# A mixture-of-experts layer on one core: bounded row transfers, paired down rows and another order of the last three experts

## The chip, the cores and the metric

The kernel runs on one core of a Trainium2 chip. The metric is device time in microseconds of one launch; the number given is the median of several runs. One further execution is recorded by the hardware profiler, and all rows below come from it.

## The reference

A decoder layer on 512 tokens of width 1024. A mixer (gated DeltaNet heads and sliding-window attention) comes first and is not touched here. Then each token is sent to 4 of 32 experts, and each expert is a clamped SwiGLU with weights of its own, all in float32:

```python
hu = xb @ w_up[e] + b_up[e]                  # 1024 -> 2048
x_glu = minimum(hu[:, :1024], 7.0)
x_lin = clip(hu[:, 1024:], -7.0, 7.0)
act = x_glu * sigmoid(1.702 * x_glu) * (x_lin + 1.0)
y = act @ w_down[e] + b_down[e]              # 1024 -> 1024
out[token] += gate[token, e] * y             # 4 experts a token
```

`w_up` is 8 MB an expert and `w_down` 4 MB, so the experts' weights are 384 MB, each used once.

## The kernel before, in words

The first 430 us or so compute the mixer, the router and the lists of rows. The experts' part follows, and there the change lies.

**Order and size.** Which expert has how many rows is known only at run time. The experts are ranked by their count, and the table `NB` gives each rank a fixed number of blocks of 32 rows: 7, 5, 5, 4, 4, 4, nine times 3, fourteen times 2, twice 1, and 4 for expert 0. `SEQ` is the order in which sizes are worked on, and `ORDER` turns it into ranks. Rows beyond a rank's blocks would go to a loop at the end (L1947 on), which did not run a pass here. An expert's rows are cut into units of 64 and, where the number of blocks is odd, one of 32 (`units`). A unit fills 128 partitions by cutting the columns in halves (64 rows) or quarters (32 rows).

**Rows in and out.** `gather` (L1685 on) makes an indirect DMA on GpSimd for each 128 rows: row numbers `gi` pick rows of `h2d` in DRAM and put them into `xg`, up to 128 partitions of 4 KB, with three buffers. Slots of the list that no token fills point at zero rows behind row 511. `turn` (L1694 on) transposes `xg` on TensorE for use as weights. At the end `put` (L1792 on) multiplies the result by gates and adds it to `out` in DRAM with an indirect DMA that accumulates, 128 pieces of 2 KB (64-row units) or 1 KB (32-row units). Unfilled slots add to rows behind row 511, which nobody reads. A scatter reads and writes `out`, so each waits until the one before it has landed; GpSimd holds the queue for that.

**Weights.** All weight loads are issued on the SP queue in chunks of 1 MB into 16 slots used in turn (`wslot`). `load_up` (L1640 on) loads eight chunks of 128 rows, where a partition receives one row of 8 KB. `load_down` (L1653 on) loads four chunks of 256 rows; chunk by chunk, partition p receives rows p and 128 + p, two runs of 4 KB. A chunk is issued when TensorE is done with the chunk that had its slot before.

**The loop.** Step q (L1904 on) loads `up(q+1)` and then `down(q)`, and on TensorE runs `up_pass(q)` (L1736 on), within it the transposes of the activations of q−1 (`turn_act`, L1769 on, after step 3) and of the rows of q+1 (`turn`, after step 5), and then `down(q−1)` (L1778 on) with its `put`. The gather for expert q+2 is issued in step q. The last step has only `down` and `put` of the last expert. TensorE, VectorE, ScalarE and SP keep the order that is written; GpSimd's is chosen by a scheduler.

`turn_act` cuts the activations' columns into pieces of 128 and transposes each, so that piece f holds rows 128f to 128f + 127 of `w_down`'s product; it has to match the order in which `load_down` put the rows on partitions.

## Time and profile before

| | us |
|---|---|
| median of 3 runs | 1517.06 (1514.83 to 1518.03) |
| the profiled execution | 1512.75 |
| its span, first to last instruction | 1510.9 |
| TensorE (PE) busy | 1384.6 (92%) |
| VectorE (DVE) busy | 563.1 (37%) |
| ScalarE (ACT) busy | 238.1 (16%) |
| GpSimd (POOL) busy | 225.4 (15%) |

Busy time counts instructions on an engine; SP's part, issuing DMAs, is not counted. Matmuls overlap one another and their ends are modelled, so a busy TensorE need not be at its peak. "DMA share" is the time that packets took as a share of 16 DMA engines; it goes over 1 where packets of several queues overlap. The granted clock is the share of full speed at which TensorE was allowed to run. Queue 1 (hardware_dynamic) carries the loads issued on SP, queue 0 (software_dynamic) what GpSimd issues, and so the gathers and scatters.

### The profile page before, as it was taken

The page shows a single profiled execution, that of the slowest core. Times are in us where ns is not written, and L with a number is a line of the kernel's source. Part 1 is how long each engine was busy: PE and PEld are TensorE (multiplying, and loading weights), DVE is VectorE, ACT ScalarE, POOL GpSimd, SP SyncE. Part 2 cuts the span into 40 slices and gives each one's busy share as a digit, 9 for nine tenths or more (in the row PEclk, how much of TensorE's full clock was granted, in tenths as well). Part 3 has the DMA queues.
Part 4 walks back from the last instruction along what each step waited for, and adds up shares of the span by engine and source line. Part 5 has one row for each costly group of instructions (what it writes and reads, how often), then busy time and mean ns, then how long its engine had stood idle before and what let it go on. Part 6 is the DMA issues. An engine that isn't in the chain of part 4 may idle for free. (4 is left out here: it accounts for less than half of the span.)

```text
span 1510.9 us, 22164 instructions
## 1 busy us (share of the span) xinstructions
PE 1384.6 (92%) x8586; PEld 595.2 (39%) x8586; DVE 563.1 (37%) x1247; ACT 238.1 (16%) x542; POOL 225.4 (15%) x181
## 2 busy tenths in 40 slices
PE   4999999999879999978999999999989999999764
PEld 3766656764433333222333333333233333343111
DVE  7865567465744213112221231233221332132110
ACT  4353354431111000000000000000000000010000
POOL 2213143101320110110011011111010111101001
PEclk9999999999979999999999999999999999999987
DMA  9656210256358999999999999999999999999996
GB/s 304 199 196 216 94 50 8 65 209 264 140 206 316 383 403 392 399 410 410 412 406 396 399 401 388 398 397 397 400 397 357 402 351 383 385 402 406 403 418 223
DMA packets 121363, 482.94 MB, mean 320 GB/s; under 512 B 10870, under 2 KB 37686, under 8 KB 88482
## 3 DMA queue, kind: packets, MB, share of 16 engines
q1 hardware_dynamic: 108226, 453.16, 76.3%
q0 software_dynamic: 11952, 25.54, 7.2%
q10 hardware_dynamic: 1072, 2.70, 0.5%
q8 instruction: 75, 1.23, 0.3%
q14 instruction: 38, 0.31, 0.1%
HBM read 464.14 MB, written 17.22 MB: 319 GB/s over the span
## 5 line engine op out<-in xcount | busy, mean ns | idle before, releaser
L1751 PE MATMUL ps_up<-we,xTe 128*64 128x512 f32 (+1 forms) x3040 | 622.0, 605 | 31.1 <-DMA we<-in_w_up_dram 27.4
L1787 PE MATMUL ps_dn<-we,aT 128*64 128x512 f32 (+1 forms) x1848 | 318.5, 535 | 31.5 <-DMA we<-in_w_down_dram 23.8
L1751 PEld LDWEIGHTS ps_up<-we,xTe 128*64 128x64 f32 (+1 forms) x3040 | 186.9, 131 | 407.0 <-issue 335.2
L1787 PEld LDWEIGHTS ps_dn<-we,aT 128*64 128x64 f32 (+1 forms) x1848 | 103.2, 129 | 248.4 <-issue 185.4
L1795 POOL DMA_INDIRECT out_dram<-yv,si x52 | 81.5, 1568 | 703.8 <-DVE yv L1794 533.1
L1703 DVE COPY xTe<-ps_xTe 128x256 f32<-128x256 f32 (+3 forms) x35 | 17.5, 500 | 308.8 <-PE ps_xTe L1702 308.8
L1775 ACT COPY aT<-ps_aT 128x512 f32<-128x512 f32 (+1 forms) x52 | 26.0, 531 | 532.7 <-PE ps_aT L1773 529.0
L1760 DVE TENSOR_TENSOR hu<-ps_up,bb 128x512 f32<-128x512 f32 (+1 forms) x52 | 32.1, 617 | 201.1 <-PE ps_up L1751 201.1
L1794 DVE SCALAR_TENSOR_TENSOR yv<-ps_dn,sg,g2p 128x512 f32<-128x512 f32 x38 | 28.5, 751 | 207.9 <-PE ps_dn L1787 207.0
L1762 ACT ACTIVATE hu<-hu 128x512 f32<-128x512 f32 (+1 forms) x52 | 29.9, 574 | 269.6 <-DVE hu L1761 269.6
L1690 POOL DMA_INDIRECT xg<-h2d,gi x35 | 33.3, 953 | 210.9 <-PE ps_xTe L1702 157.7
L317 PE MATMUL ps_ch<-hhi,wih 128*128 128x512 f32 x128 | 58.9, 460 | 0.0
L317 PE MATMUL ps_ch<-hl,wih 128*128 128x512 f32 x128 | 51.0, 399 | 0.0
L317 PE MATMUL ps_ch<-hhi,wl 128*128 128x512 f32 x128 | 50.8, 396 | 0.0
L1711 DVE STREAM_SHUFFLE bb<-bias 128x1024 f32<-128x1024 f32 (+1 forms) x44 | 48.7, 1134 | 0.1
L1703 ACT COPY xTe<-ps_xTe 128x256 f32<-128x256 f32 (+3 forms) x35 | 15.2, 434 | 170.6 <-PE ps_xTe L1702 170.6
L1702 PEld LDWEIGHTS ps_xTe<-cst,xg 64*128 64x128 f32 (+3 forms) x280 | 24.8, 144 | 30.8 <-issue 25.3
L1161 PE MATMUL ps_y<-wod,oT 128*128 128x512 f32 x64 | 35.2, 641 | 0.0
L1702 PE MATMUL ps_xTe<-cst,xg 64*128 64x64 f32 (+3 forms) x280 | 30.8, 252 | 3.2 <-PEq L1745 1.8
L317 PEld LDWEIGHTS ps_ch<-hhi,wih 128*128 128x128 f32 x128 | 24.2, 189 | 23.2 <-issue 18.0
L1142 PE MATMUL ps_y<-wos,oS 128*128 128x512 f32 x64 | 33.3, 613 | 0.0
L1766 DVE SCALAR_TENSOR_TENSOR act<-act,hu 128x512 f32<-128x512 f32 (+1 forms) x52 | 32.2, 620 | 1.8
(391 smaller groups left out, 1337.2 us busy)
## 6 DMA issues: line engine op xcount, KB each, us to landing
we<-in_w_up_dram SPq DMA_DIRECT2D x256, 1024.0 KB
we<-in_w_down_dram SPq DMA_DIRECT2D x128, 1024.0 KB
wa<-in_w_ada_dram SPq DMA_DIRECT2D x16, 512.0 KB
wi<-in_w_in_dram SPq DMA_DIRECT2D x8, 1024.0 KB
wl<-in_w_ada_dram SPq DMA_DIRECT2D x12, 512.0 KB
oS<-in_w_ada_dram SPq DMA_DIRECT2D x10, 512.0 KB
LL<-in_w_ada_dram SPq DMA_DIRECT2D x10, 512.0 KB
wt<-in_w_in_dram SPq DMA_DIRECT2D x4, 776.0 KB
```

Of the source, the lines that this page charges most:

```text
L317: TE.matmul(acc, lhsT=w[a], rhs=x_[b], start=start and q == 0, stop=stop and q == 2)
L1142: TE.matmul(a, lhsT=oS[:, j, P * i:P * i + P], rhs=wo[j][:, 512 * hf:512 * hf + 512], start=(j == 0), stop=(j == 3))
L1161: TE.matmul(a, lhsT=state["oT"][:, j, P * i:P * i + P], rhs=wo[4 + j][:, 512 * hf:512 * hf + 512], start=(j == 0), stop=(j == 3))
L1690: state["gather"] = G.indirect_dma_start(out=xg[:rows_], out_offset=None, in_=h2d, in_offset=bass.IndirectOffsetOnAxis(ap=gidx(g)[:rows_], ...
L1702: TE.transpose(pt[:, k, :rows_], xg[:rows_, 512 * hf + P * k:512 * hf + P * k + P], ident[:rows_, :rows_])
L1703: state["turned", hf] = (S.copy if hf else V.tensor_copy)(xt_[:, 4 * hf:4 * hf + 4, :rows_], pt[:, :, :rows_])
L1711: V.stream_shuffle(bbs[w].rearrange("p h n -> p (h n)"), b[w], [0] * 32)
L1751: TE.matmul(t[w * j:w * j + w], lhsT=lhsT, rhs=rhs, start=(k == 0), stop=(k == KT - 1))
L1760: V.tensor_tensor(g, pg, bbs[w][:, 0], op=OP.add)
L1766: V.scalar_tensor_tensor(l, l, 1.0, g, op0=OP.add, op1=OP.mult)
L1787: TE.matmul(py[u][w * j:w * j + w, 0:m], lhsT=aT[u][:, kt % nf, w * (kt // nf):w * (kt // nf) + w], rhs=wd[kt][:, m * j:m * j + m], start= ...
L1795: G.indirect_dma_start(out=outv[u[1]], out_offset=bass.IndirectOffsetOnAxis(ap=sidx, axis=0), in_=yv, in_offset=None, compute_op=OP.add)
```

## The change

There are four edits.

1. `SEQ` ends in 3, 1, 1 and no longer in 1, 3, 1: the expert of three blocks is worked on before both experts of one block.
2. The gather is bounded to rows 0 to 511 and the scatter to pieces of these rows. What points beyond is left out without an error. Since the partitions of `xg` that receive no row would hold old data, a memset of `xg` on GpSimd stands ahead of each gather.
3. `load_down` puts rows 2p and 2p + 1 of a chunk on partition p, one run of 8 KB.
4. `turn_act` picks the matching columns for each transpose: every second column of a group of 256, first the even ones, then the odd ones.

```diff
-SEQ = [..., 5, 2, 2, 1, 3, 1]
+SEQ = [..., 5, 2, 2, 3, 1, 1]
...
     def load_down(dn):
...
-            nc.sync.dma_start(t, dn[P * kt:P * kt + 256].rearrange("(f p) n -> p f n", p=P))
+            nc.sync.dma_start(t, dn[P * kt:P * kt + 256].rearrange("(p f) n -> p f n", f=2))
...
+            G.memset(xg[:rows_], 0.0)
             state["gather"] = G.indirect_dma_start(
-                out=xg[:rows_], out_offset=None, in_=h2d, in_offset=bass.IndirectOffsetOnAxis(ap=gidx(g)[:rows_], axis=0))
+                out=xg[:rows_], out_offset=None, in_=h2d, in_offset=bass.IndirectOffsetOnAxis(ap=gidx(g)[:rows_], axis=0),
+                bounds_check=T - 1, oob_is_err=False)
...
     def turn_act(u, l):
...
-        for a in range(0, m, P):
-            TE.transpose(pt[:, a:a + P], l[:, a:a + P], ident)
+        lv = l.rearrange("p (g q f) -> p g f q", f=2, q=P)
+        for a in range(m // P):
+            TE.transpose(pt[:, P * a:P * a + P], lv[:, a // 2, a % 2], ident)
...
         G.indirect_dma_start(out=outv[u[1]], out_offset=bass.IndirectOffsetOnAxis(ap=sidx, axis=0),
-                             in_=yv, in_offset=None, compute_op=OP.add)
+                             in_=yv, in_offset=None, compute_op=OP.add, bounds_check=T * D // m - 1, oob_is_err=False)
```

## Rows read from the trace of the kernel before

**Rows 1.** The page: DMA busy in 40 slices (tenths), queue 0's packets, MB, share.
```profile
DMA  9656210256358999999999999999999999999996
...
q0 software_dynamic: 11952, 25.54, 7.2%
```

**Rows 2.** Stretches: us, busy PE, PEld, DVE, ACT, POOL, granted clock, DMA share, GB/s.
```profile
488.00:1121.00 633.00, 601.22 (x3314) 201.00 (x3311) 160.11 (x311) 42.01 (x81) 67.14 (x52) 0.99 1.02 399
1121.00:1250.00 129.00, 128.03 (x699) 44.52 (x694) 39.12 (x96) 8.54 (x16) 15.73 (x13) 1.00 0.98 373
1250.00:1396.00 146.00, 141.72 (x726) 52.50 (x718) 38.19 (x73) 11.21 (x23) 18.78 (x14) 1.00 1.03 394
1396.00:1490.00 94.00, 69.55 (x412) 19.38 (x414) 16.97 (x39) 4.83 (x11) 6.21 (x4) 0.85 1.02 412
```

**Rows 3.** Waits of PE, 488 to 1121 us: total us, times, longest.
```profile
PE ps_dn L1787 <- DMA we<-in_w_down_dram: 16.7, 12, 3.8
PE ps_up L1751 <- DMA we<-in_w_up_dram: 12.7, 17, 1.7
```

**Rows 4.** Waits of PE, 1396 to 1490 us.
```profile
PE ps_up L1751 <- DMA we<-in_w_up_dram: 14.7, 14, 1.8
PE ps_dn L1787 <- DMA we<-in_w_down_dram: 7.2, 8, 1.5
```

**Rows 5.** Waits of the SP queue for TensorE, 1121 to 1396 us.
```profile
SPq L1649 <- PE ps_dn L1787: 27.8, 10, 7.3
...
SPq L1649 <- PE ps_up L1751: 24.0, 13, 8.6
```

**Rows 6.** Queue 0 (packets, MB, share) in 488:1121, 1250:1396 and 1396:1490.
```profile
q0 software_dynamic: 6480, 14.55, 9.7%
...
q0 software_dynamic: 1712, 3.28, 10.3%
...
q0 software_dynamic: 576, 0.79, 4.8%
```

**Rows 7.** Stretches of up chunks (first) and of down chunks; columns as rows 2.
```profile
1466.30:1473.70 7.40, 4.07 (x24) 0.52 (x24) 0.00 (x0) 0.00 (x0) 0.00 (x0) 0.79 1.00 420
1445.80:1453.30 7.50, 4.08 (x48) 1.43 (x48) 3.63 (x9) 0.42 (x1) 0.00 (x0) 0.79 1.04 426
1414.30:1421.80 7.50, 5.81 (x24) 1.45 (x24) 0.87 (x3) 0.00 (x0) 0.00 (x0) 1.00 1.03 425
```

**Rows 8.** Timeline of POOL and DVE at the end: start, us, what, idle before.
```profile
1488.23 1.55 POOL L1795 DMA_INDIRECT out_dram<-yv,si  x1 [30.52 <-DVE yv L1794]
1495.73 1.55 POOL L1795 DMA_INDIRECT out_dram<-yv,si  x1 [5.95 <-DVE yv L1794]
1500.00 1.55 POOL L1795 DMA_INDIRECT out_dram<-yv,si  x1 [2.71 <-DMA out_dram<-yv,si]
...
1495.18 0.48 DVE L1794 SCALAR_TENSOR_TENSOR yv<-ps_dn,sg,g2s 128x256 f32<-128x256 f32 x1 [6.83 <-PE ps_dn L1787]
```

**Rows 9.** Landing times: the scatter of L1795, then the gather into xg.
```profile
DMA to landing us min/median/max: 3.8/9.0/10.3
...
DMA to landing us min/median/max: 6.4/8.7/11.7
```

**Rows 10.** Transposes: L934 (strided source) and L1773 (contiguous); ns min/median/max.
```profile
L934 PE MATMUL ps_tm<-cst,kT x16: 272/273/329, 117.0 to 286.6; 128*128 128x128 f32 x16
...
L1773 PE MATMUL ps_aT<-cst,act x180: 272/273/476, 465.9 to 1487.8; 128*128 128x128 f32 x180
```

**Rows 11.** POOL's memsets of the bias tiles; POOL's first gather in the timeline.
```profile
L1681 POOL MEMSET bias<- x4: 539/752/967, 440.4 to 442.2; 128x512 f32 x2, 128x1024 f32 x2
...
431.39 1.05 POOL L1690 DMA_INDIRECT xg<-h2d,gi  x1 [7.51 <-DVE gi L1537]
```

**Rows 12.** GB/s of all DMA from 1480 to 1511 us in 40 slices.
```profile
GB/s 423 423 423 407 423 423 418 423 412 407 418 418 433 362 328 304 185 95 21 11 0 21 11 137 32 21 0 0 40 120 9 0 11 0 0 0 0 0 0 0
```

**Rows 13.** Timeline of PE: eight products of the last expert's up pass, twice.
```profile
1468.77 1.07 PE L1751 MATMUL ps_up<-we,xTe 128*32 128x512 f32 x8 [1.35 <-DMA we<-in_w_up_dram]
1471.21 1.93 PE L1751 MATMUL ps_up<-we,xTe 128*32 128x512 f32 x8 [1.38 <-DMA we<-in_w_up_dram]
```

## The prediction

> **What bounds the kernel now.** The page comes first: from the fourteenth of its forty slices on, the experts' part, the DMA row stands at 9 [rows 1]. The table by stretch says the same in numbers: DMA share 1.02 from 488 to 1121 us, 0.98 to 1250, 1.03 to 1396, 1.02 to 1490, while TensorE is busy for 601 of 633, 128 of 129, 142 of 146 and 70 of 94 us [rows 2]. Both engines are nearly full, so the waits decide who leads where. Up to 1121 us TensorE waits 16.7 + 12.7 = 29.4 us for weights [rows 3]. From 1121 to 1396, with the expert of seven blocks, that list has no wait for weights; the DMA queue waits instead for TensorE to free slots (27.8 + 24.0 us are its largest such rows) [rows 5]. From 1396 on TensorE waits again, 14.7 + 7.2 us [rows 4]: the weight stream sets the end. So what shortens DMA work counts in full only after about 1250 us, where the queue was last throttled (share 0.98 before it); earlier it counts where TensorE waits, and between 1121 and 1250 not at all. After the stream comes a tail of its own, in the timeline: the last product is read out at 1495.18, but its scatter starts at 1500.00, because the scatter of 1495.73 has to land first, and that one had waited for the scatter of 1488.23 [rows 8].

> **The order of the last experts.** Before, the last expert but one has three blocks and so two scatters, chained by their landings; the last expert's is third in the chain. Then the last but one has one block and one scatter. It starts about four down chunks before the last one's, four times 1.05 MB at 425 GB/s = 9.9 us [rows 7], and a scatter lands 9.0 us after issue in the median, 10.3 at most [rows 9]: at most 0.4 us are left to wait. The last scatter then starts where the readout ends, at 1495.73 and not at 1500.00: −4.3 us. Two things are late next. The three-block expert's second scatter now runs before the end of the stream. Queue 0 spends 4.5 us on 576 packets from 1396 to 1490 [rows 6], four scatters of 128 rows and 16 completions, 1.1 us each; this one has rows of half a pair, so I take 0.5 us. And TensorE has two experts of one block at the end: the same eight products took 1.07 us in one chunk and 1.93 in the next [rows 13], with the granted clock at a mean of 0.85 in that stretch [rows 2]; the last chunk of before took 1.07, so up to 0.9 us come on, taken as 0.4. Together −3.4, between −4.3 and −1.9. The weights themselves are the same bytes, and TensorE's blocks are the same number.

> **The bounded transfers.** The table NB gives 90 blocks, 2880 rows; 512 tokens times 4 choices are at most 2048 rows in use, so at least 832 of 2880, 28.9%, are moved for nothing, by gathers and by scatters. Queue 0, which carries both, takes 9.7% of 633 us = 61.4 us up to 1121, 10.3% of 146 = 15.0 us, and 4.8% of 94 = 4.5 us of all 16 engines' time [rows 6]. 28.9% of the last two is 5.6 us. Early it is 17.7 us, less than the 29.4 us that TensorE waits there [rows 3]. Bounds: nothing, if a skipped row costs as much as a moved one or if no engine that matters is relieved; 5.6 + 17.7 = 23.3 us if all counts. I take 5.6, the late part whole and the early part at nothing: TensorE's waits up to 1121 are 5% of that stretch, so most of what is saved there fills slots that the queue then waits for [rows 5], and what does get through I set against rows that are shared unevenly among the engines.

> Bounding may make the instruction or the making of its descriptors longer; no row has a bounded one. The nearest rows are the unbounded ones' landing times, 8.7 us for a gather and 9.0 for a scatter in the median [rows 9]. Both only lie on the path at two places: the first gather, which TensorE waits for at the start, and the last scatter. I take 0; the ends are no cost and a doubling, 17.7 us for the two, and below nothing is possible too, as fewer rows land sooner, in the range's 1 us.

> The 35 memsets go to GpSimd, up to 0.97 us each [rows 11]. The gather then waits for the memset ahead of it, and scatters queue behind both. The first has 7.5 us of idle GpSimd ahead of it [rows 11]; the others are issued up to two experts ahead, and an expert is 12 chunks of 1.05 MB at 420 GB/s [rows 7], 30 us, against a landing of 11.7 at most [rows 9]. Cost 0 behind that cover; were it gone, 1 us per gather that TensorE waits for.

> **Down rows in pairs.** A down chunk becomes 128 runs of 8 KB, as an up chunk is. Rows 7 compare stretches of one kind: up chunks come at 420 GB/s with share 1.00, down chunks at 426 and 425 with 1.04 and 1.03. By bytes delivered nothing is won. By share per byte a down chunk costs 1.04/426 against 1.00/420, 2.5% more; the ten late experts' 42 MB take 2.38 us per MB, 100 us, so that would be 2.5 us. I take 0, the rate being what TensorE sees; ends 0 and −2.5. [...]

> The transposes of the activations now read every second element as weights. L934 already transposes with a strided source (two heads interleaved), in 273 ns in the median, as L1773 does on contiguous data [rows 10]. So 0; the far end, twice the time for 180 of them, would be 49 us and has no row behind it.

> **Sum.** −3.4 − 5.6 = −9.0 us. The profiled execution took 1512.75 us (span 1510.9 and 1.85 around it), 4.3 below the median of 1517.06; it becomes 1503.8, the median 1508.1, said as 1508. The forecast's own range is 1503 to 1512. A difference under 0.2%, 3 us, is about what a measurement of this kernel can't tell from none.

> **Rivals.**
> *Only the tail gains.* The rows in use are the first of every transfer. If each engine gets a run of neighbouring rows, the first engines keep all of theirs, and the stream waits for them. For it: at the end of the stream the rate falls in steps from 433 to 95 GB/s over some 4 us [rows 12], so the engines do not finish together. Against it: nothing tells which rows go to which engine. The time: 1517.06 − 3.4 = 1513.7, just on the line of 0.2%. It is also the time if a skipped row still costs its slot in the queue, the case that bounding does not do what it says. [...] Chance 0.25.

> *The early savings count as well.* TensorE's 29.4 us of waiting [rows 3] fall by about half of the 17.7 us saved there, and the whole second half shifts. −3.4 − 5.6 − 8 = −17, 1500. For it: the waits are there; against it: slots fill. Chance 0.13.

> *Slower: bounded transfers land late.* If the check of every row makes a bounded transfer land x us later, the first gather and the last scatter add 2x on the path, and it decides from 2x above 9.0, x = 4.5, half of today's landing. Doubled, +17.7 − 9.0: 1525.8. For it: POOL's transfers take 9 us for little data, so making them is the larger part; against it: one comparison a row. Chance 0.12.

> **How the numbers follow.** Forecast 0.50, tail only 0.25, early too 0.13, slower 0.12. Tail only falls on both sides of the line, half and half: faster 0.50 + 0.13 + 0.12 = 0.75, same 0.13, slower 0.12. The range takes in the forecast, the early case and the tail case with its own spread: 1498 to 1516; outside it lie the slower case and a part of the early one.

> **What would show it.** The tail: two scatters after the last but one expert's readout and no idle GpSimd "DMA out_dram" before the last. The bound: of 2880 gathered and 52 × 128 = 6656 scattered rows 28.9% go, some 2750 of queue 0's 11952 packets [rows 1]. If its packets are as many as before, or TensorE's waits after 1396 stay at 22 us with fewer packets, the second term falls. Down rows: packets under 8 KB fall by 128 × 256 = 32768 for the down rows alone, and stretches of down chunks keep 425 GB/s. The forecast is wrong if TensorE's part ends where it did, or if landing times rise above 9 us.

## The result, and the profile after

| | before | changed |
|---|---|---|
| median of 4 runs each, us | 1515.94 (1511.09 to 1518.03) | 1491.98 (1486.96 to 1492.84) |
| ratio, 95% interval | | 0.9843 (0.9818 to 0.9868) |
| profiled execution; its span | 1512.75; 1510.9 | 1486.96; 1485.2 |

The change takes 24 us off, 1.6%; forecast were 9 us, and the measured time is 6 us below the range. Two of the edits did more than was forecast of them: the bounded transfers and the paired down rows.

The page of the changed kernel, DMA packets and queues; against it the same line of before (queue 0 of before is in [rows 1]):

```profile
DMA packets 104980, 476.16 MB, mean 321 GB/s; under 512 B 13992, under 2 KB 39556, under 8 KB 55714
...
q1 hardware_dynamic: 91842, 453.16, 77.0%
q0 software_dynamic: 11952, 18.75, 5.4%
```

```profile
DMA packets 121363, 482.94 MB, mean 320 GB/s; under 512 B 10870, under 2 KB 37686, under 8 KB 88482
...
q1 hardware_dynamic: 108226, 453.16, 76.3%
```

Packets under 8 KB are 32768 fewer: the down rows, as forecast. Queue 0 has 6.8 MB less and 5.4% instead of 7.2%, but exactly as many packets. Packets under 512 B are 3122 more. The router's choices for the reference's inputs leave 832 of 2880 gathered rows and 2290 of 6656 scattered pieces without a token, and that is 3122: what is left out keeps its packet. In the packet records a scattered piece becomes a packet of 8 bytes (2290 more of these on queue 0) and a gathered row one of 4 bytes (832 more); their median time is 9 ns, against 176 ns for a piece of 2 KB, 101 for one of 1 KB and 159 for a row of 4 KB.

The changed kernel by stretch (columns as [rows 2]), then what TensorE waited for from 488 to 1121 us and from 1396 to 1470, then queue 0 (packets, MB, share) from 1250 to 1396 and from 1396 to 1470:

```profile
488.00:1121.00 633.00, 609.78 (x3362) 208.02 (x3356) 159.95 (x312) 42.52 (x82) 90.08 (x73) 1.00 1.01 400
1121.00:1250.00 129.00, 127.69 (x696) 45.53 (x693) 37.71 (x91) 9.16 (x18) 19.19 (x17) 1.00 0.95 372
1250.00:1396.00 146.00, 141.81 (x723) 52.90 (x721) 40.39 (x77) 10.93 (x22) 21.81 (x17) 1.00 1.02 408
1396.00:1470.00 74.00, 56.51 (x366) 16.13 (x370) 13.74 (x33) 3.84 (x10) 6.21 (x4) 0.82 1.00 409
```

```profile
PE ps_dn L1792 <- DMA we<-in_w_down_dram: 11.7, 11, 3.1
PE ps_up L1755 <- DMA we<-in_w_up_dram: 9.0, 12, 1.8
...
PE ps_up L1755 <- DMA we<-in_w_up_dram: 10.5, 10, 1.9
...
PE ps_dn L1792 <- DMA we<-in_w_down_dram: 2.2, 4, 0.7
```

```profile
q0 software_dynamic: 1665, 1.78, 6.0%
...
q0 software_dynamic: 636, 0.42, 3.4%
```

TensorE's waits for weights fall from 29.4 to 20.7 us early [rows 3] and from 21.9 to 12.7 late [rows 4], 18 us in all. Late, queue 0 moves 2.20 MB instead of 4.07 [rows 6], 46% less and not 28.9%, at about as many packets (2301 and 2288): the last experts of the order have the emptiest blocks. Next come three points in time, the first down product of all (on PE, 475.55), the first of the expert of seven blocks (1184.24) and the last readout (on DVE, 1473.54), and the last scatter (on POOL):

```profile
475.55 1.46 PE L1792 MATMUL ps_dn<-we,aT 128*64 128x512 f32 x6
...
1184.24 1.51 PE L1792 MATMUL ps_dn<-we,aT 128*64 128x512 f32 x6
...
1473.54 0.48 DVE L1799 SCALAR_TENSOR_TENSOR yv<-ps_dn,sg,g2s 128x256 f32<-128x256 f32 x1 [10.05 <-PE ps_dn L1792]
...
1474.30 1.55 POOL L1800 DMA_INDIRECT out_dram<-yv,si  x1 [8.99 <-DVE yv L1799]
```

```profile
478.13 1.46 PE L1787 MATMUL ps_dn<-we,aT 128*64 128x512 f32 x6
...
1197.08 1.51 PE L1787 MATMUL ps_dn<-we,aT 128*64 128x512 f32 x6
```

The second fence is before. Between these points: 718.95 us before, 708.69 after, 10.3 less early; then to the last readout 298.10 (to 1495.18, [rows 8]) and 289.30, 8.8 less late. The last scatter now starts right behind the readout and waits for no landing: from readout to the end of the span 15.7 us before and 11.7 now, 4.1 less. The part ahead of the experts varies by some us from one execution to the next (the first gather of the executions recorded here was issued between 426 and 434 us), so lengths between such points compare better than times from the start. The choice of the first point matters too: counted from the first gather (431.39 [rows 11] and 427.16) the early gain is 8.6 us.

### The profile page after: what moved, and what is told of

It reads as the page before. It is cut to its first block, busy times and chain, and to the rows that moved or that the text cites. A ratio compares the mean times of both kernels' runs of the same rounds, so it can differ in the third digit from the quotient of the medians.

```text
span 1485.2 us, 22293 instructions
## 1 busy us (share of the span) xinstructions
PE 1379.4 (93%) x8586; PEld 599.5 (40%) x8586; DVE 563.7 (38%) x1247; ACT 237.7 (16%) x542; POOL 261.1 (18%) x216
## 3 DMA queue, kind: packets, MB, share of 16 engines
q0 software_dynamic: 11952, 18.75, 5.4%
## 5 line engine op out<-in xcount | busy, mean ns | idle before, releaser
L1755 PE MATMUL ps_up<-we,xTe 128*64 128x512 f32 (+1 forms) x3040 | 621.0, 605 | 22.7 <-DMA we<-in_w_up_dram 19.7
L1692 POOL MEMSET xg<- 64x1024 f32 (+3 forms) x35 | 37.1, 1080 | 188.9 <-PE ps_xTe L1706 188.6
L1778 PEld LDWEIGHTS ps_aT<-cst,act 128*128 128x128 f32 x180 | 24.3, 208 | 29.3 <-issue 25.6
L1778 PE MATMUL ps_aT<-cst,act 128*128 128x128 f32 x180 | 31.2, 304 | 2.3 <-DVE act L1770 1.9
```

Of the source, the lines that this page charges most:

```text
L1692: G.memset(xg[:rows_], 0.0)
L1755: TE.matmul(t[w * j:w * j + w], lhsT=lhsT, rhs=rhs, start=(k == 0), stop=(k == KT - 1))
L1778: TE.transpose(pt[:, P * a:P * a + P], lv[:, a // 2, a % 2], ident)
```

## The experiments

The theory to begin with, called A in the expectations: rows that are left out free the DMA engines for the weight stream, early as well as late. Its rivals and successors are told there. Ratios are to the kernel before, measured beside each group of runs.

### Each edit alone

```diff
# bound only: memset, bounds on gather and scatter, all else as before
# pairs only: load_down "(p f) n -> p f n" and turn_act's strided columns
# order only: SEQ = [..., 5, 2, 2, 3, 1, 1]
# bounded, none left out: the changed kernel with
-                bounds_check=T - 1, oob_is_err=False)
+                bounds_check=ROWS - 1, oob_is_err=False)
...
-                             ... bounds_check=T * D // m - 1, oob_is_err=False)
+                             ... bounds_check=ROWS * D // m - 1, oob_is_err=False)
```

Expected of the bounds alone: 

> The kernel before with the bounded transfers and the memset alone. Theory A (the rows left out free the DMA engines, and that counts early and late): 15 to 20 us faster than before, ratio 0.987 to 0.990; queue 0 keeps its 11952 packets and moves 18.75 MB in place of 25.54. Theory B (the paired down rows carry a large part): 8 to 12 us faster.

Of the pairs alone: 

> The kernel before with the paired down rows and the strided transposes alone. Theory A: 0 to 3 us faster, ratio 0.998 to 1.000, as down chunks come at the same GB/s either way. Theory B (the packets of 8 KB save 9 us of all engines' time by queue 1's share): 6 to 9 us faster, ratio 0.994 to 0.996.

Of the order alone: 

> The kernel before with the last three experts of 3, 1, 1 blocks alone. Both theories: the last scatter no longer waits for a landing, 3 to 4.3 us faster, ratio 0.997 to 0.998. If the order also moves work of TensorE out of the last stretch, more than 5 us.

Of the changed kernel with bounds that leave nothing out: 

> The changed kernel with bounds so wide (640 rows) that no row is left out; memsets, pairs and order stay. Theory A: loses what the left-out rows give, 15 to 20 us slower than the changed kernel, so 4 to 8 us faster than before (ratio 0.995 to 0.997). Theory C (bounding or the memset itself costs time that the result hides): as slow as before or slower.

| run | ratio to before (interval) | us |
|---|---|---|
| bounds alone | 0.9888 (0.9870 to 0.9906) | −16.9 |
| pairs alone | 0.9976 (0.9963 to 0.9988) | −3.6 |
| order alone | 0.9975 (0.9962 to 0.9989) | −3.8 |
| all, none left out | 0.9972 (0.9960 to 0.9983) | −4.2 |

The us are the ratio's distance from 1 times the median of before beside these runs, 1513.2. The first three add up to −24.3, the whole change. With bounds set so wide that no row is left out, queue 0 moves 25.54 MB as before, and 4.2 us remain (2.6 to 6.1): the gain of the bounds is that of the rows left out. Pairs and order alone add up to 7.4; whether the memsets and the bounding itself cost some of the 3.2 between, or noise does, these runs don't separate. In the profile of the bounds alone:

```profile
482.28 1.46 PE L1789 MATMUL ps_dn<-we,aT 128*64 128x512 f32 x6
...
1194.56 1.51 PE L1789 MATMUL ps_dn<-we,aT 128*64 128x512 f32 x6
...
1485.47 0.48 DVE L1796 SCALAR_TENSOR_TENSOR yv<-ps_dn,sg,g2s 128x256 f32<-128x256 f32 x1 [7.47 <-PE ps_dn L1789]
```

712.28 us early, 6.7 less than before, and 290.91 late, 7.2 less. In the five profiled kernels here that leave nothing out the early length is 717.6 to 720.6 us, so the 6.7 are more than their spread. Counted from the first gather, issued at 433.00, the early part is 761.6 us against 765.7, 4.1 less (764.9 to 767.8 in the five). So between a third and a half of what this execution gained came early. It was the slowest of its kernel's five, 6.2 us above their median.

### Scatters and gathers apart; half of the pieces more

The last two of the four kernels below leave out half of the scattered pieces on top, by adding 8192 to their index (JROW32 as JROW64), so that their sums are missing from the output.

```diff
# scatters alone: bounds_check on the scatter of before, nothing else
# gathers alone: memset and bounds_check on the gather of before, nothing else
# upper half left out (every second: p[:, None] % 2 == 1)
-        ("JROW64", 2 * (T + ...) + p[:, None] // 64),
+        ("JROW64", 2 * (T + ...) + p[:, None] // 64 + 8192 * (p[:, None] >= 64)),
```

Scatters alone: 

> The kernel before, with the bounds on the scatters alone. Theory A (rows left out free DMA engines for the weight stream, wherever they are, and memset and wait on GpSimd cost nothing): of the two kinds of rows left out, the scattered pieces have about two thirds of the DMA time (2290 pieces of 1 to 2 KB read and written, against 832 rows of 4 KB), so of the 17 us of both bounds 10 to 12 come from here: ratio 0.992 to 0.9935. Rival B (what counts is the late part and the landing of the last scatter): 3 to 6 us, 0.996 to 0.998.

Gathers alone: 

> The kernel before, with memset and bounds on the gathers alone. Theory A: the other third, 5 to 7 us, ratio 0.9955 to 0.997, and with the scatters alone it adds up to the 17 us of both. Rival C (the memsets ahead of the gathers give back what the gathers save): within 2 us of before, 0.9987 to 1.0013.

Upper half: 

> The changed kernel, with the scattered pieces of partitions 64 to 127 left out as well: their sums are missing from the output, about half of the 4366 pieces that are still in use. Theory A with engines that share every transfer evenly: another 8 to 11 us faster than the changed kernel, ratio to before 0.977 to 0.979, and the same as the twin that leaves out every second partition. Rival (neighbouring rows go to one engine, so that half of the engines keep all of theirs and the stream waits for them): 0 to 3 us faster, 0.982 to 0.984, and the twin is 8 to 11 us faster.

Every second: 

> The changed kernel, with the scattered pieces of the odd partitions left out as well: their sums are missing from the output. Theory A with engines that share every transfer evenly: 8 to 11 us faster than the changed kernel, 0.977 to 0.979, like the twin that leaves out partitions 64 to 127. If rows are dealt to the engines in turn, this one relieves half of the engines alone: 0 to 3 us, 0.982 to 0.984, and the twin 8 to 11. If neighbouring rows go to one engine, this one has 8 to 11 and the twin 0 to 3.

The scatters alone came to 0.9938 (0.9916 to 0.9960), −9.4 us, the gathers to 0.9966 (0.9951 to 0.9980), −5.1: both parts count, and the memsets do not take back what the gathers save. What the memsets cost by themselves was not run. Without the upper half, 0.9864 (0.9838 to 0.9890): nothing gained on the changed kernel's 0.9843, though queue 0 moves 14.57 MB instead of 18.75. Without every second one, the same bytes, 0.9769 (0.9747 to 0.9792), 11 us less. How the two streams end shows why. The last 12 us before the last weight packet, in stretches of 4 us (DMA share and GB/s are the last two columns); first the upper half left out, then every second:

```profile
1466.50:1470.50 4.00, 2.64 (x29) 0.86 (x22) 0.00 (x0) 0.00 (x0) 0.00 (x0) 0.71 0.70 291
1470.50:1474.50 4.00, 3.51 (x30) 1.33 (x34) 0.48 (x1) 0.37 (x1) 1.55 (x1) 0.50 0.44 180
1474.50:1478.50 4.00, 1.84 (x28) 0.47 (x20) 0.00 (x0) 0.00 (x0) 0.00 (x0) 0.93 0.24 85
```

```profile
1448.80:1452.80 4.00, 2.63 (x34) 1.03 (x26) 0.21 (x1) 0.00 (x0) 0.00 (x0) 0.82 1.01 428
1452.80:1456.80 4.00, 2.85 (x34) 1.01 (x32) 0.28 (x1) 0.37 (x1) 1.55 (x1) 0.75 0.94 393
1456.80:1460.80 4.00, 2.14 (x20) 0.59 (x16) 0.00 (x0) 0.00 (x0) 0.00 (x0) 0.67 0.54 201
```

In the first the rate falls to less than half, at a share of 0.44, 8 us before the end, though its last chunk had been issued by 1459.1 us, so that no slot was missing: by that share, an estimate, about half of the engines have finished, and the stream ends with the others. As I read it, what was taken from some engines only was not gained. I took this to mean that eight neighbouring partitions go to one engine, the first engine being the fullest.

### Rows dealt by eights, another order, contiguous transposes

```diff
# dealt by eights: partition 8j + k of a group takes row 8k + j
+def dealt(p, w):
+    r = p % w
+    return p - r + w // 8 * (r % 8) + r // 8
...
+            V.tensor_copy(t.rearrange("e (b j k) -> e b j k", j=w // 8, k=8),
+                          ten.rearrange("e (b k j) -> e b j k", j=w // 8, k=8))
# other order
+SEQ = [4, 1, 4, 3, 2, 2, 3, 2, 5, 3, 3, 2, 2, 3, 4, 3, 2, 2, 2, 2, 2, 7, 2, 3, 2, 3, 5, 2, 4, 3, 1, 2]
# contiguous transposes: before, with load_down "(p f) n -> p f n" alone
```

By eights: 

> The changed kernel, with the rows of every group of 64 (of 32 in a last half group) dealt over the partitions: row 8k + j of a group sits on partition 8j + k, so that the rows in use are spread over all DMA engines instead of filling the first ones. As many rows are left out as in the changed kernel. Theory A2 (eight neighbouring partitions go to one engine, and the weight stream waits for the fullest one): by 135 ns a scattered piece and 190 ns a gathered row the fullest engine has 82 us of these rows in the changed kernel and 72 us here, so 4 to 10 us faster than the changed kernel, ratio to before 0.977 to 0.982. Rival (only the mean over the engines counts): as the changed kernel, 0.983 to 0.986, and the two copies on VectorE before the first gather can cost up to 1 us.

Other order: 

> The changed kernel with another order of all experts, in which light and heavy ones are spread so that by a model of stream and products TensorE hardly waits; the last two have one and two blocks. If the waits of both engines for each other are what is left to gain (TensorE 11.7 + 9.0 + 10.5 us for weights, the queue 23.2 + 20.9 + 18.2 us for slots), 5 to 15 us faster than the changed kernel, ratio to before 0.974 to 0.981. Rival: the weight stream is the bound all the way, and another order only moves the waits: 0.983 to 0.987.

Both: 

> Rows dealt and the other order together. If both work and on different waits, 8 to 20 us faster than the changed kernel, 0.971 to 0.979; where TensorE has no waits left, the second adds nothing to the first, and the time is that of the better of the two.

Contiguous transposes: 

> The kernel before, with the down rows loaded in pairs but the activations transposed from contiguous columns: they are paired with the wrong rows of the down weights, at the same work otherwise. The kernel with pairs and strided transposes had 0.9976. If reading every second column costs nothing on the path, the same, 0.996 to 0.999; if the strided reads, some 69 ns longer each, delay TensorE where it sets the pace, faster than that by up to 180 of them, 12 us: 0.990 to 0.996.

The dealing lost: 0.9903 (0.9881 to 0.9925), 9 us slower than the changed kernel. My map of engines had to be wrong. The other order came to 0.9835 (0.9810 to 0.9860), as the changed kernel: its rival held, the waits only moved (TensorE waited 37 us for weights from 488 to 1470, against 34). Both together, 0.9870 (0.9849 to 0.9891). With contiguous transposes the pairs had 0.9976 (0.9960 to 0.9992), the same as with strided ones: no cost of the strided reads on the path can be seen, though these intervals leave room for up to some 3 us.

### Which engines hold the stream

```diff
# lower half: + 8192 * (p[:, None] < 64); partitions 32 to 63: p[:, None] // 32 == 1; 0 to 31: p[:, None] // 32 == 0
# reversed: row r of a group of w rows sits on partition w - 1 - r, nothing missing
```

Lower half: 

> The changed kernel, with the scattered pieces of partitions 0 to 63 left out as well, the mirror of the upper half: their sums are missing from the output, as many pieces as there. Theory A3 (eight neighbouring partitions go to one engine, and an engine of the first eight is the slowest of the stream, whatever it carries besides): the upper half gave 0 to 3 us, this gives 8 to 15 us against the changed kernel, ratio to before 0.974 to 0.980. Rival D (not the engine counts but how many rows in use follow one another, so that only alternate rows give room): both halves alike, 0.983 to 0.987.

Partitions 32 to 63: 

> The changed kernel, with the scattered pieces of partitions 32 to 63 left out as well (887 in use, by the counts of rows per expert): their sums are missing from the output. Theory A3, which takes engines 6 and 7 for the slowest since dealing the rows gave these two more of them and cost some 7 us: 5 to 12 us faster than the changed kernel, 0.976 to 0.981. Rival A2 (the fullest engine, 0, sets it): 0 to 2 us, 0.983 to 0.986.

Partitions 0 to 31: 

> The changed kernel, with the scattered pieces of partitions 0 to 31 left out as well (1296 in use, the fullest four engines): their sums are missing from the output. Theory A3: 0 to 3 us, 0.983 to 0.986. Rival A2 (the fullest engine sets it): 5 to 10 us, 0.977 to 0.981.

Reversed: 

> The changed kernel, with the rows of every group of 64 (of 32 in a last half group) in reverse, so that the rows left out lie on the first partitions of each half instead of the last: as many left out, nothing missing from the output. Theory A3 (engines 6 and 7 are the slowest): they lose the relief of 20 to 35 us that the changed kernel gives them, so 10 us slower than it or more, near the kernel before, 0.990 to 0.998. Rival A2: as the changed kernel within 3 us, since the fullest engine has as much as there. Rival D (rows in use that follow one another): the same.

The first three leave further sums out of the output. Measured: 0.9826 (0.9811 to 0.9842), 0.9827 (0.9810 to 0.9844), 0.9834 (0.9816 to 0.9852) and, reversed, 0.9842 (0.9823 to 0.9862). None differs from the changed kernel by more than 3 us. As I read it, no single engine holds the stream by itself, since neither half gains more than 3 us when it is relieved (0.9826 and 0.9864 against 0.9843), and here it did not matter at which end of a group the empty rows lie (0.9842).

The map came from the last scatter of each run, which runs when no weights do. The last expert has 12 rows in use, on partitions 0 to 11, 32 to 43, 64 to 75 and 96 to 107. In the packet records each such scatter has 16 closing packets of 4 bytes, and where pieces are left out some of the 16 come early. The records name no engine; I read each closing packet as that of one engine, and the early ones as those of engines without rows (times from the scatter's first packet):

```
kernel                  pieces in use   closing packets
before                       128        16 at 0.82 to 1.29 us
changed                       48        10 by 0.26, 6 at 0.81 to 1.28
upper half left out           24        13 by 0.26, 3 at 0.82 to 1.16
32 to 63 left out             36        10 by 0.26, 3 at 0.52 to 0.54, 3 at 1.01 to 1.25
every second left out         24        10 by 0.27, 6 at 0.55 to 0.84
dealt by eights               48         8 by 0.26, 8 at 0.67 to 1.05
```

### Rows dealt by fours

```diff
 def dealt(p, w):
     r = p % w
-    return p - r + w // 8 * (r % 8) + r // 8
+    return p - r + 8 * (w // 32 * (r % 4) + r // 32) + r // 4 % 8
...
```

By fours: 

> The changed kernel, with the rows of every group dealt over the engines as the last scatters of the earlier runs show them to share a transfer: the first 64 partitions go to eight engines, the other 64 to the other eight, four neighbouring partitions at a time in turn. Row 8k + j of a group goes to the j-th of eight engines. By the counts of rows per expert, the fullest engine has 335 scattered pieces in use in the changed kernel, 346 in the kernel that dealt the rows by eights, 290 here, at a mean of 273 (416 before the change). Theory A4 (the fullest engine sets the stream, some 120 ns a piece): 45 pieces, 5 us, less up to 1 us for the two or three copies before the first gather: 3 to 7 us faster than the changed kernel, ratio to before 0.979 to 0.983. Rival (dealing rows costs in itself, as the 7 us of the other dealing): slower than the changed kernel by 3 us or more, above 0.986.

With the other order: 

> Rows dealt by fours, and the other order of the experts as well. The order alone gave 0.9835 and with the rows dealt by eights 0.987. Theory A4: as much faster than the order alone as dealing by fours makes the changed kernel, 3 to 7 us: 0.978 to 0.982. If TensorE has become the bound by then: no more than the better of the two.

Alone it came to 0.9838 (0.9813 to 0.9863), within 1 us of the changed kernel where 3 to 7 were expected; with the other order to 0.9807 (0.9783 to 0.9831), 1484.52 us, the fastest kernel here with nothing left out of the output. Against the dealing by eights it is 9.8 us faster, and 9.5 with the other order, as the map has it. The closing packets of its last scatter agree as well: by the map its 48 pieces in use lie on all 16 engines, and all 16 packets come late, at 0.33 to 0.71 us. Against the undealt kernels it is 0.8 and 4.2 us faster. With the map, the counts of rows give the scattered pieces in use on the fullest engine and in the mean:

| kernel | fullest | mean | ratio |
|---|---|---|---|
| before | 416 | 416 | 1 |
| scatters alone | 335 | 273 | 0.9938 |
| changed | 335 | 273 | 0.9843 |
| reversed | 335 | 273 | 0.9842 |
| lower half left out | 335 | 136 | 0.9826 |
| upper half left out | 335 | 136 | 0.9864 |
| 0 to 31 left out | 335 | 192 | 0.9834 |
| 32 to 63 left out | 335 | 217 | 0.9827 |
| every second left out | 169 | 138 | 0.9769 |
| dealt by eights | 346 | 273 | 0.9903 |
| dealt by fours | 290 | 273 | 0.9838 |

Queue 0's share fell from 7.2% of 1510.9 to 6.1% of 1503.4 us with the scatters alone, 17.1 us per engine for 143 pieces in the mean, an estimate of 120 ns each. The fullest engine lost 81, 9.7 us; measured were 9.4 (6.0 to 12.7). The mean would have given 17.1. Six kernels with 335 lie within 6 us of one another, whatever their mean. For every second piece the count gives 20 us and 11 came: a part of the reason may be that TensorE sets the pace at times (DMA share 0.89 from 1121 to 1250 us). From eights to fours it gives 6.7 for the 9.8 and 9.5 measured. Against the changed kernel both dealt kernels lie 5 to 8 us above this line. For fours that is within the noise: the intervals leave some 5 us either way, and from the first gather to the last readout its profile has 1042.3 us against 1046.4, 4.1 less where the count gives 5.4. For eights it is not (1053.6), and why stays open. It is not the code that deals the rows: the reversed kernel has such copies and products before the first gather (GpSimd stood idle 7.71 us ahead of it there, 7.90 in the kernel dealt by eights, 7.12 in the changed one) and is as fast as the changed one. How gathers of 64 and 32 rows are shared among the engines wasn't measured.

## Why the prediction was wrong

**The step that failed** is the sizing of the bounded transfers: "I take 5.6, the late part whole and the early part at nothing". Alone they gave 16.9 us (14.2 to 19.7), within the bounds of 0 to 23.3. Two choices in it were wrong.

*The early part at nothing.* I argued that a slot filled sooner only makes the queue wait for TensorE [rows 5]. The profile of the bounds alone shows 6.7 us early (4.1 from the first gather): TensorE waited 29.4 us there [rows 3], which means that the stream, not TensorE, set the pace in pieces of that stretch, and such pieces can get shorter. [rows 5], on which the argument leans, are of 1121 to 1396 us, where TensorE had no wait for weights. From 488 to 1121 us the SP queue's list before has, as its longest wait and its longest for TensorE:

```profile
SPq L1649 <- DMA we<-in_w_down_dram: 157.4, 69, 4.1
...
SPq L1649 <- PE ps_up L1751: 24.6, 17, 4.5
```

Summed, the queue waited 306 us for DMA transfers, nearly all of its own weights, and 114 for TensorE. With the bounds alone the latter is 127 (with the order alone 110): part of the 17.7 us reckoned for the early part did fill slots, as argued, but not all. That the wait was 5% of the stretch said how often the stream led there, not that its savings were lost: 6.7 us came. The rival that counted the early savings as well had this right, with 8 us and a chance of 0.13.

*28.9% everywhere.* That is the mean over all gathered rows; of the scattered pieces 34.4% went (2290 of 6656), as a row of a 32-row unit has four pieces, and late it was 46% of queue 0's bytes. From 1250 us on the order has experts whose last blocks are hardly used. The counts follow from the reference's inputs and could have been worked out ahead, stretch by stretch. Late came 7.2 us instead of 5.6.

**"Only the tail gains"** fits the runs in that the stream waits for the engines that keep their rows, and was wrong on which rows these are. Half of the pieces taken away, by the map those of eight engines, gave nothing (0.9864 against 0.9843); every second one, by the map from all sixteen, gave 11 us (0.9769). But by the map the rows in use aren't one run per engine: with fours in turn, the empty end of a group reaches every engine, and the fullest lost 81 of 416 pieces, not none. "Nothing tells which rows go to which engine" held for the trace as I had read it; the closing packets of a lone bounded scatter point to it, and with that map the scatters' part of the term is a matter of counting: 335 of 416 pieces on the fullest engine, an estimate of 9.7 us where 9.4 were measured.

**"If its packets are as many as before … the second term falls"** was a wrong test. The packets are as many (11952) and the term grew (16.9 us for 5.6); the bytes and the time of queue 0 were the rows to ask for.

**The down rows in pairs**, taken at 0 with ends 0 and −2.5, gave 3.6 us (1.8 to 5.6). Queue 1's time is 76.3% of 1510.9 = 1152.8 us before and, for pairs alone, 75.9% of 1508.5 = 1145.0 us:

```profile
q1 hardware_dynamic: 91842, 453.16, 75.9%
```

Rates of three short stretches [rows 7] don't resolve a difference of 0.7%, and only the late chunks were counted. The packet records show one: on queue 1 before, a packet of 4 KB takes 159 ns in the median and one of 8 KB 309, so two of 4 KB take 9 ns more than one of 8. The pairs make 16384 packets of 8 KB out of 32768 of 4 KB; at 9 ns each, over 16 engines, that is, as an estimate, 9.2 us, beside the 7.8 us less on queue 1 and the 3.6 us in time. Why two packets take longer than one is not shown.

**What held.** The order: −3.4 forecast, −3.8 measured alone (−1.7 to −5.7), and the tail shows the mechanism, −4.1 of the −4.3; the 0.9 us of costs beside it are too small to tell. The memsets: POOL is busy for 261 us instead of 225, gathers wait for the memset ahead of them for 0.3 us each at most, and TensorE's list of waits has one for a gather, 2.5 us at the first, where before it has none. The landings: the scatter's median stays at 9.0 us and the gather's is 8.5 [rows 9], so "bounded transfers land late" fell:

```profile
DMA to landing us min/median/max: 3.8/9.0/10.8
...
DMA to landing us min/median/max: 4.0/8.5/11.8
```

The transposes: no cost on the path that shows, though the row on which I took 0 misled. Line 934's source, called strided in [rows 10], is not: `kTv` holds its columns in the order (n e c), and each transpose there takes 128 neighbouring ones, so that the row compared contiguous with contiguous. The weight loads for the transposes of the activations, which became strided, did become longer; first before, then the changed kernel:

```profile
L1773 PEld LDWEIGHTS ps_aT<-cst,act x180: 137/140/230, 465.9 to 1487.7; 128*128 128x128 f32 x180
```

```profile
L1778 PEld LDWEIGHTS ps_aT<-cst,act x180: 193/209/220, 461.0 to 1463.0; 128*128 128x128 f32 x180
L1778 PE MATMUL ps_aT<-cst,act x180: 280/284/389, 461.0 to 1463.1; 128*128 128x128 f32 x180
```

The load takes 209 ns in the median instead of 140, the product 284 instead of 273 [rows 10]. The kernel with contiguous reads was not faster.

## What to carry to other kernels

Where two engines lead in turns, a saving can count, in part at least, wherever the lagging one is waited for, as the 6.7 us did early in the profile of the bounds alone, where TensorE had waited 29.4 us for weights; size it by the waits it can shorten, stretch by stretch, and with the data's own shares there. Where small transfers run beside a stream, as the scatters do here, count what the fullest engine has: the 81 pieces that it lost, by the map, gave an estimate of 9.7 us, the mean's 143 one of 17.1, and 9.4 were measured. Spreading the empty rows over all engines should then pay, but the dealing by fours gained 0.8 us alone and 4.2 with the other order, so that is not shown clear of noise. Bounding the indirect transfers saved bytes (18.75 MB on queue 0 instead of 25.54) and engine time (5.4% instead of 7.2%), not packets (11952 both times), and no landing time (the scatter's median 9.0 us both times).

## What the runs showed of the hardware that was not expected

- What a bounded indirect transfer left out still made a packet: 11952 on queue 0 with and without 3122 rows and pieces, the difference being 2290 packets of 8 bytes (scatter) and 832 of 4 (gather), 9 ns in the median.
- The closing packets of the last scatter, in seven kernels, agree with a map by which a scatter from 128 partitions is shared by fours of partitions in turn over eight engines per half (3 to 16 of the 16 late, as many as the map gives). By this map 2183 pieces fewer on eight engines gave nothing (0.9864 against 0.9843), 2166 fewer on all sixteen 11 us (0.9769), as if the weight stream waited for the fullest engine.
- In the last scatter, which runs alone, most pieces of 1 KB took 102 ns, and a few, somewhat more than there are late closing packets, 210 to 650 ns (packet records; 101 and 22 of the 128 before, 41 and 7 of the 48 in the changed kernel).
- Less data did not land sooner here: the scatter's median is 9.0 us with 6656 pieces and with 4366.
